# Two gate projections per layer leave the dense phase and join the queue of filler work; modulation sums start earlier; filler budgets change

## The chip, the cores and the metric

The kernel runs on one core of a Trainium2 chip. The metric is the device time of one execution in microseconds (us). TensorE (PE in the rows) does the matrix products, ScalarE (ACT) the activations, casts and exponentials, VectorE (DVE) the elementwise work and the scans, GpSimd (POOL) and SyncE (SP) issue DMAs; ACT issues some too.

## The reference, cut to what matters

Two layers, each on x of 1024 tokens and 1024 channels. A layer modulates a normalised input by sums over `c`, makes one wide projection, runs two attention mixers over it, gates each mixer's output with a SiLU gate, projects, mixes and adds to the residual stream.

```python
mod = jax.nn.silu(c) @ ada_w + ada_b
shift, scale, gate = jnp.split(mod, 3, axis=-1)
h = rms_norm(x, norm_g) * (1 + scale[:, None]) + shift[:, None]
proj = h @ w_in
(sb_q, sb_k, sb_v, sb_z, n_q, k_c, v_c, k_s, v_s, k_w, v_w, n_z, n_g, m_a, m_b) = jnp.split(proj, ...)
a = stick_breaking_attention(heads(sb_q, 8), heads(sb_k, 8), heads(sb_v, 8))
a = a.reshape(B, S, 512) * jax.nn.silu(sb_z)
b = native_sparse_attention(q, kc, vc, ks, vs, kw, vw, n_g)     # 8 heads of 64, 2 key heads
b = b * jax.nn.silu(n_z)
y = jax.nn.sigmoid(m_a) * (a @ w_proj_a) + jax.nn.sigmoid(m_b) * (b @ w_proj_b)
return x + gate[:, None] * (y @ w_out)
```

Stick-breaking weights are a product over the later keys: with z the scaled score, the weight of a key is sigmoid(z) times the product of sigmoid(-z) over the keys between it and the query. The part of the change that matters is `sb_z`: 512 channels whose SiLU multiplies the stick-breaking output, and `mod`, the modulation sums.

## The kernel before

Every float32 product runs as three passes of a split operand (hi times hi, hi times lo, lo times hi), so a unit of a projection (128 channels, 512 tokens, contraction 1024) is 24 matmuls of 128x512: lines L194, L196 and L198 in `mm3_gen`. Four such units (two channel halves `u`, two token halves `half`) make a weight group of 256 columns.

A layer has four stages.

- **Early** (`early`): dense projections whose outputs the sparse attention needs, in code order: compressed keys and values, keys, then a loop of eight token tiles that makes values and branch gates (24 matmuls of 280 columns each, called the v loop below), queries, and at its end the loop over `z` with four groups of SiLU gates (16 units; groups 0 and 1 gate the sparse attention, 2 and 3 the stick-breaking heads). A gate unit is 24 matmuls, a Sigmoid on ACT (L824), a product on DVE (L825) and a store to `SZ` in DRAM. The loop also carries the modulation sums: `mod_part` cuts a sum into eight steps, each a load of 512 KB of `ada_w` (L359, tile `ada`, two buffers) and one DVE instruction over 128x1024 (L362 for the first, L364 for the others). Layer 0 has 24 steps (its own residual gate and the next layer's shift and scale), layer 1 has eight. Two steps go behind each gate unit. When the loop is done, `gate_rows` (L411 on PE, L412 on DVE) and `cols` (L373 on PE, L388 to L391 on DVE) turn the sums into the gate and the modulation vectors.
- **Sparse attention** (`nsa`): a software pipeline of jobs, one for a head and query pair. PE's bursts of a job alternate with queued projection work, the filler: `pump(us)` emits matmuls of the queue `self.fill` until the given amount is spent. The amounts by query pair are written by hand (`nsa_us`, `cmp_us`, and `start_us` before the first job).
- **Stick-breaking** (`sb`): the same pipeline over eight heads with four query pairs each (m0 to m3, 256 to 1024 keys), amounts `sb_us`. On ACT the two sigmoids of the scores (L1239, L1240), on DVE the scan over keys (L1243) and the product (L1244), then PE transposes (L879), ACT and DVE split them (wh, wl) and PE multiplies them with the values (L898, L899).
- **Output** (`output`): loads the mixers' outputs (`AD`, L1333, issued by POOL), splits them, y units (gated projections), output projection, residual, and the norm of the next layer.

The queue before holds 14 groups per layer: queries, keys and values of the stick-breaking heads (six groups) and the eight groups of the mixing gates `m`. By the budgets' own unit, sparse attention spends 8 x (1.97 + 4.16 + 5.85 + 7.05 + 1.48) + 3, about 167 us of it, stick-breaking 8 x 15.02 + 3, about 123 us, against 14 x 20.45 = 286 us of queue (the code reckons a group as 96 matmuls of 0.213 us): the queue before runs out about 4 us before the last job ends. `output` begins when the queue is empty and the last job has been emitted; the scheduler of the framework, not the code alone, decides how far its first products move up among the last head's.

The order within each engine is fixed before the run. An instruction behind a waiting one on the same engine waits too.

Of the kernel before, what the change touches and what calls it, by code (L numbers as in the profile page):

```python
"""Hybrid decoder trunk (stick-breaking attention + native sparse attention) on one Trainium2 core.

float32 products run as three float32r passes: every operand is split exactly into hi + lo
(12 significant bits each), and hi*hi + hi*lo + lo*hi is accumulated in float32 PSUM.  Attention
operands are stacked along the contraction ([hi; lo]) so that two passes carry all four products.
"""
# [14 lines left out]
P = 128  # L21
# [16 lines left out]
def make_consts():  # L38
    """Constants that depend on shapes alone, packed along the free dimension of 128 partitions."""
# [48 lines left out]
class Trunk:  # L88
    def __init__(self, tc, I, O, depth=2, dbg=None):
# [7 lines left out]
        # amount of projection work that is put between the bursts of an attention job, by query pair  # L97
        self.nsa_us = (1.97, 4.16, 5.85, 7.05)
        self.sb_us = (1.34, 2.87, 4.77, 6.04)
        self.cmp_us = 1.48  # L100
        self.start_us = 3.0
        self.tail = 0.15
        # how far dependent transposes are put off
# [11 lines left out]
    # ---------------------------------------------------------------- helpers  # L115
# [17 lines left out]
    def split(self, src, hi, lo):  # L133
        """hi = round12(src) on ScalarE, lo = src - hi on VectorE; src in PSUM or SBUF, float32."""
        nc = self.nc
        nc.scalar.copy(hi, src)  # L136
        nc.vector.tensor_tensor(lo, src, hi.bitcast(F32), ALU.subtract)  # L137

    def rsqrt(self, pool, ss, n, inv, tag, on_pool=False):
        """1/sqrt(ss * inv + EPS) by Newton steps; ss [rows, n]."""  # L140
# [21 lines left out]
    # ---------------------------------------------------------------- weights  # L162
    def load_raw(self, srcs, ncols):
        """srcs(kc) -> list of (DRAM AP [128, 2, ...], column slice) of contraction chunks kc, kc+1."""
# [13 lines left out]
    def split_raw(self, raw):  # L178
        """Tile [128, hi/lo, 2, columns]."""
        n = raw.shape[2]  # L180
        w = self.tl(self.wpool, [P, 2, 2, 280], F32R, "w", bufs=self.wb)
        self.split(raw, w[:, 0, :, :n], w[:, 1, :, :n])
        return w

    def load_group(self, srcs, ncols):
        """The four tiles of a weight group."""
        return [self.split_raw(raw) for raw in self.load_raw(srcs, ncols)]

    def mm3_gen(self, ps, pairs, cost):
        """Three-pass product over pairs ((lhs_hi, lhs_lo), (rhs_hi, rhs_lo)), matmul by matmul."""  # L190
# [21 lines left out]
    def t_unit(self, w, u, half, act, ks=range(KD)):  # L212
        """[128 columns, 512 tokens] = w columns^T @ act^T for one half of the tokens."""
# [4 lines left out]
    def n_unit(self, w, t, act, ncols):  # L218
        """[128 tokens, ncols] = act tokens @ w."""
# [4 lines left out]
    def n_units(self, w, ts, act, ncols):  # L224
        """n_unit of several token tiles, the last chunk of the contraction after the others of all."""
# [9 lines left out]
    # ---------------------------------------------------------------- order of the tensor engine  # L235
    def tick(self, us):
        """us of tensor-engine work have been emitted: emit the deferred work that is due."""
# [4 lines left out]
    def defer(self, us, f):  # L242
        """Emit f once us of tensor-engine work have gone by, so that its operands are ready."""
# [18 lines left out]
    def take(self, ahead=1):  # L262
        """Weights of the next group of the plan; the loads of those that follow are emitted as well."""
# [4 lines left out]
    # ---------------------------------------------------------------- filler: projections run between bursts  # L268
    def pump(self, us):
        """Emit about us microseconds of queued projection work."""  # L270
# [16 lines left out]
    def run_jobs(self, jobs):  # L287
        """jobs: (A bursts, B bursts, us).  The A bursts of a job go between the B bursts of the one before,
        and queued projection work after every burst."""
# [1163 lines left out]
```

## Time and profile before

| | before |
| --- | --- |
| device time, median of 3 | 2231.28 us (2230.01 to 2231.57) |
| span of the profiled execution | 2229.4 us |
| PE busy | 2131.1 us, 96% |
| DVE busy | 1572.0 us, 71% |
| ACT busy | 1129.2 us, 51% |
| PE clock granted in 40 slices | full in nearly all |

The span is that of one profiled execution; the time of the median is 1.9 us more. The rows below come from that execution. A window row gives each engine's busy time in a stretch and the granted clock of TensorE as a share of full speed (1.00 is 2.4 GHz). Matmul ends are modelled, so PE shown busy for a whole window need not be at its best pace; the start of one matmul to the next is the better measure.

### The profile page before, as it was taken

What the parts mean: (1) busy time and instruction counts of PE and PEld (TensorE: products, weight loads), DVE (VectorE), ACT (ScalarE), POOL (GpSimd) and SP (SyncE); (2) the same over time, 40 slices, a digit from 0 to 9 for tenths busy, and PEclk for the clock granted to TensorE, in tenths of its full rate; (3) what the DMA queues carried; (4) which work ended last, traced back from release to release, by engine and by line L of the source; (5) the groups of instructions that cost most, each with busy time, mean ns of one, the idle gap of its engine ahead of it and who ended that gap; (6) DMA issues with size and microseconds to landing.
All of it is one profiled execution on the core that took longest, in us unless ns stands there. A gap on an engine that the chain in (4) does not pass through costs nothing.

```text
span 2229.4 us, 36753 instructions
## 1 busy us (share of the span) xinstructions
PE 2131.1 (96%) x13128; PEld 1841.4 (83%) x13128; DVE 1572.0 (71%) x3714; ACT 1129.2 (51%) x2481; POOL 60.2 (3%) x226
## 2 busy tenths in 40 slices
PE   3999999999999999999999998999999999999999
PEld 3899778988887777789889986889898877777899
DVE  5857558868765877877765852887788487787643
ACT  4533147656665655663443421665666465656410
POOL 2100000000000000000010000000000000001000
PEclk8999999999999999999999999999999999999999
DMA  7435862252116445275455355322522364534433
GB/s 286 131 124 180 250 156 79 88 151 96 66 49 165 127 125 137 86 246 174 159 149 160 97 189 141 94 86 86 142 91 67 92 154 112 149 100 168 150 123 102
DMA packets 239256, 297.04 MB, mean 133 GB/s; under 512 B 21993, under 2 KB 186721, under 8 KB 239073
## 3 DMA queue, kind: packets, MB, share of 16 engines
q1 hardware_dynamic: 198560, 250.65, 36.6%
q10 hardware_dynamic: 36224, 29.37, 5.1%
q0 software_dynamic: 4288, 14.68, 2.0%
q8 instruction: 103, 1.69, 0.3%
q14 instruction: 81, 0.66, 0.1%
HBM read 206.28 MB, written 83.89 MB: 130 GB/s over the span
## 4 chain that ended last, share of the span: by engine, by line
PE 66%; DVE 17%; DMA 7%; issue 5%; ACT 3%; POOL 1%; SPq 0%; ACTq 0%; DVEq 0%; POOLq 0%
PE proj L194 15%; PE proj L198 15%; PE proj L196 15%; PE tr L879 6%; DVE C L1243 4%; PE av L899 4%; PE av L898 3%; PE sc L866 3%; PE sc L867 3%; DVE wl L137 2%; DVE E L1244 2%; DMA ada<-in_ada_w 2%; DVE w L137 2%; DMA kk<-QK 1%; DMA q<-QK 1%
## 5 line engine op out<-in xcount | busy, mean ns | idle before, releaser
L194 PE MATMUL proj<-acthi,w 128*128 128x512 f32 x1312 | 536.9, 409 | 1.3 <-ACT acthi L136 0.7
L196 PE MATMUL proj<-actlo,w 128*128 128x512 f32 x1312 | 536.8, 409 | 0.5 <-DVE actlo L137 0.5
L198 PE MATMUL proj<-acthi,w 128*128 128x512 f32 x1312 | 536.2, 409 | 0.7 <-DVE w L137 0.7
L136 ACT CAST w<-raw 128x512 fp32r<-128x512 f32 (+1 forms) x296 | 183.4, 622 | 230.1 <-PE proj L198 119.0
L137 DVE TENSOR_TENSOR wl<-tr,wh 128x512 fp32r<-128x512 f32 (+2 forms) x432 | 256.6, 610 | 40.8 <-ACT wh L136 38.4
L194 PEld LDWEIGHTS proj<-acthi,w 128*128 128x128 f32 x1312 | 249.4, 190 | 42.1 <-ACT acthi L136 1.6
L196 PEld LDWEIGHTS proj<-actlo,w 128*128 128x128 f32 x1312 | 249.4, 190 | 39.0 <-DVE actlo L137 1.9
L198 PEld LDWEIGHTS proj<-acthi,w 128*128 128x128 f32 x1312 | 249.0, 190 | 37.9 <-DVE w L137 1.2
L137 DVE TENSOR_TENSOR w<-raw,w 128x512 fp32r<-128x512 f32 (+1 forms) x296 | 202.2, 688 | 81.9 <-ACT w L136 79.8
L136 ACT CAST wh<-tr 128x512 fp32r<-128x512 f32 (+2 forms) x432 | 221.2, 527 | 76.1 <-PE tr L879 70.7
L899 PE MATMUL av<-wl,V 128*128 128x256 f32 (+1 forms) x864 | 217.5, 285 | 7.6 <-DVE wl L137 7.3
L194 PE MATMUL proj<-w,acthi 128*128 128x256 f32 (+1 forms) x768 | 221.2, 288 | 2.2 <-DVE s L137 1.7
L198 PE MATMUL proj<-w,actlo 128*128 128x256 f32 (+1 forms) x768 | 221.0, 288 | 0.0
L196 PE MATMUL proj<-w,acthi 128*128 128x256 f32 (+1 forms) x768 | 219.8, 286 | 0.0
L898 PE MATMUL av<-wh,V 128*128 128x256 f32 (+1 forms) x864 | 216.8, 271 | 1.2 <-DVE o L917 0.5
L879 PE MATMUL tr<-ident,E 128*128 128x128 f32 x1152 | 187.3, 276 | 23.7 <-DVE E L1244 23.0
L1243 DVE TENSOR_TENSOR_SCAN C<-C 128x128 f32<-128x128 f32 (+7 forms) x128 | 172.5, 1349 | 53.0 <-ACT C L1239 52.4
L879 PEld LDWEIGHTS tr<-ident,E 128*128 128x128 f32 x1152 | 139.2, 140 | 67.4 <-DVE E L1244 35.0
L899 PEld LDWEIGHTS av<-wl,V 128*128 128x128 f32 x864 | 162.7, 188 | 31.1 <-DVE wl L137 19.3
L866 PE MATMUL sc<-kk,q 128*128 128x512 f32 (+3 forms) x512 | 176.8, 346 | 8.6 <-DVE mx L1079 4.1
L867 PE MATMUL sc<-kk,q 128*128 128x512 f32 (+3 forms) x512 | 175.5, 343 | 0.0
L898 PEld LDWEIGHTS av<-wh,V 128*128 128x128 f32 x864 | 163.0, 189 | 14.0 <-ACT wh L136 3.9
(247 smaller groups left out, 3898.2 us busy)
## 6 DMA issues: line engine op xcount, KB each, us to landing
raw<-in_w_in SPq DMA_DIRECT2D x168, 256.0 KB, 2.9
ada<-in_ada_w SPq DMA_DIRECT2D x48, 512.0 KB, 5.3
kk<-QK SPq DMA_DIRECT2D x48, 512.0 KB, 9.0
q<-QK ACTq DMA_DIRECT2D x64, 256.0 KB, 4.0
QK<-s SPq DMA_DIRECT2D x32, 512.0 KB, 3.0
MD<-sz SPq DMA_DIRECT2D x64, 256.0 KB, 2.6
QK<-s SPq DMA_DIRECT2D x48, 256.0 KB, 3.3
VD<-s SPq DMA_DIRECT2D x48, 256.0 KB, 2.1
```

Of the source, the lines that this page charges most:

```text
L136: nc.scalar.copy(hi, src)
L137: nc.vector.tensor_tensor(lo, src, hi.bitcast(F32), ALU.subtract)
L194: nc.tensor.matmul(ps, lh, rh, start=(x == 0), stop=False)
L196: nc.tensor.matmul(ps, lh, rl, start=False, stop=False)
L198: nc.tensor.matmul(ps, ll, rh, start=False, stop=(x == n - 1))
L866: nc.tensor.matmul(ps, q, k[:, 0, c0:c1], start=True, stop=False)
L867: nc.tensor.matmul(ps, q, k[:, 1, c0:c1], start=False, stop=not masks)
L879: nc.tensor.transpose(pt[:, x * P:x * P + P], b, self.ident)
L898: nc.tensor.matmul(ps[:, c:d], lhsT, hi[:, a:b], start=(first and x == 0), stop=False, skip_group_check=True)
L899: nc.tensor.matmul(ps[:, c:d], lhsT, lo[:, a:b], start=False, stop=(last and x == n - 1), skip_group_check=True)
L1243: nc.vector.tensor_tensor_scan(rev, rev, rev, 1.0, ALU.mult, ALU.bypass)
L1244: nc.vector.tensor_tensor(e[:, 0:nk], e[:, 0:nk], c[:, 1:nk + 1], ALU.mult)
```

## The change

Three edits, one diff (docstrings and comments are blanked in the changed file, so line numbers shift by a few; L824 becomes L840, L1000 becomes L1008, L866 becomes L874, L879 becomes L887).

1. `early` makes only two of the four gate groups. The other two stand first in `self.fill`, as kind "sb" (they have to be done before stick-breaking begins).
2. The filler budgets grow, and the start budget of the sparse attention is 13 us where it was 3; stick-breaking keeps 3.
3. The steps of the modulation sums begin before the v loop: one step per token tile there, then two per gate unit as before, over eight units.

```diff
-        self.nsa_us = (1.97, 4.16, 5.85, 7.05)
-        self.sb_us = (1.34, 2.87, 4.77, 6.04)
-        self.cmp_us = 1.48
-        self.start_us = 3.0
+        self.nsa_us = (2.1, 4.5, 6.3, 7.6)
+        self.sb_us = (1.8, 3.8, 6.2, 7.8)
+        self.cmp_us = 1.6
+        self.start_us = 13.0
...
-    def run_jobs(self, jobs):
+    def run_jobs(self, jobs, start):
...
-            us = jobs[n - 1][2] if n else self.start_us
+            us = jobs[n - 1][2] if n else start
...
             w = self.take()
+            steps = []
+            self.gate, gate_rows = self.mod_gate(l, pool, steps)
+            if l + 1 < self.depth:
+                cols = self.mod_ab(l + 1, pool, steps)
+
+            def mod_steps(n, ins):
+                with tc.issue_after(ins.ins):
+                    for f in steps[:n]:
+                        f()
+                del steps[:n]
+
             for t in range(NT):
                 ps = self.n_unit(w, t, act, 280)
-                self.store_v(ps, t, 8)
+                ins = self.store_v(ps, t, 8)
                 nc.scalar.activation(self.G[:, t, :], ps[:, 256:280], AF.Sigmoid)
+                mod_steps(1, ins)
...
-            for z in range(4):
+            for z in range(2):
                 w = self.take()
-                if z == 0:
-                    steps = []
-                    self.gate, gate_rows = self.mod_gate(l, pool, steps)
-                    if l + 1 < self.depth:
-                        cols = self.mod_ab(l + 1, pool, steps)
                 for u in range(2):
                     for half in range(2):
-                        ps = self.t_unit(w, u, half, act)
-                        s = self.tl(self.stage, [P, 512], F32, "sz")
-                        nc.scalar.activation(s, ps, AF.Sigmoid)
-                        ins = nc.vector.tensor_tensor(s, ps, s, ALU.mult)
-                        with tc.issue_after(ins.ins):
-                            for f in steps[:2]:
-                                f()
-                        del steps[:2]
-                        r0 = z * 256 + u * 128
-                        nc.sync.dma_start(self.SZ[r0:r0 + P, half * 512:half * 512 + 512], s)
+                        mod_steps(2, self.silu_gate(self.t_unit(w, u, half, act), z * 256 + u * P, half))
...
+    def silu_gate(self, ps, r0, half):
+
+        nc = self.nc
+        s = self.tl(self.stage, [P, 512], F32, "sz")
+        nc.scalar.activation(s, ps, AF.Sigmoid)
+        ins = nc.vector.tensor_tensor(s, ps, s, ALU.mult)
+        nc.sync.dma_start(self.SZ[r0:r0 + P, half * 512:half * 512 + 512], s)
+        return ins
...
-            self.run_jobs(jobs)
+            self.run_jobs(jobs, self.start_us)
...
-            self.run_jobs(jobs)
+            self.run_jobs(jobs, 3.0)
...
+                    if what == "z":
+                        self.silu_gate(ps, r0 + u * P, half)
+                    elif what == "qk":
...
+        for z in range(2):
+            self.fill.append(("sb", t_group("z", 512 + z * 256)))
```

DVE at the end of layer 0's early stage, before (rows of the last gate units; `sz` is a gate unit's product, `acc` a step of the sums, `gate` and `Acol` what is made of them):

```order
L364 SCALAR_TENSOR_TENSOR acc_388_2324<-ada_2801,silu_c_86,acc_388_2324 128x1024 [waits DMAHW2_49,DVE_49]
L825 TENSOR_TENSOR sz_2850<-proj_2825,sz_2850 128x512 [waits DMAHW7_49,Activation_49]
L825 TENSOR_TENSOR sz_2879<-proj_2854,sz_2879 128x512 [waits DMAHW4_49,Activation_49]
L825 TENSOR_TENSOR sz_2908<-proj_2883,sz_2908 128x512 [waits DMAHW7_49,Activation_49]
...
L825 TENSOR_TENSOR sz_2937<-proj_2912,sz_2937 128x512 [waits DMAHW0_49,Activation_49]
L412 TENSOR_TENSOR gate_2311<-proj_2941,gate_2311 128x512 [waits PE_49]
```

And in the changed kernel:

```order
L841 TENSOR_TENSOR sz_2659<-proj_2634,sz_2659 128x512 [waits DMAHW4_49,Activation_49]
L364 SCALAR_TENSOR_TENSOR acc_213_1096<-ada_2663,silu_c_86,acc_213_1096 128x1024 [waits DMAHW0_49,DVE_49]
L412 TENSOR_TENSOR gate_1083<-proj_2669,gate_1083 128x512 [waits PE_49]
L364 SCALAR_TENSOR_TENSOR acc_213_1096<-ada_2666,silu_c_86,acc_213_1096 128x1024 [waits DMAHW2_49,DVE_49]
L412 TENSOR_TENSOR gate_1083<-proj_2672,gate_1083 128x512 [waits PE_49]
L388 SCALAR_TENSOR_TENSOR Acol_1087<-proj_2675,vcols_1093 128x8 [waits PE_49]
```

Before, four gate units' products stand behind the last step of the sums; now the last two steps stand behind the last gate unit's product, and the gate's own instructions between and behind them.

ACT at the opening of layer 0's sparse attention, before (`sz` of the last gate unit is done; V and q are loads; `cs`, `E` and `ew` are exponentials, `s` evictions of queries and keys in the queue):

```order
L936 DMA q_2983<-QK_120_589 64x4x256 x2
L936 DMA q_3063<-QK_120_589 64x4x256 x2
L1000 ACT_TABLE_LOAD
L1000 ACTIVATE cs_2991<-cs_2991 128x32
L1091 ACTIVATE E_3067,rs_3070<-E_3067,mx_3069 128x128
L136 CAST s_529_3141<-proj_3027 128x512
```

And in the changed kernel:

```order
L840 ACTIVATE sz_2780<-proj_2755 128x512
L944 DMA q_2848<-QK_120_589 64x4x256 x2
L1008 ACT_TABLE_LOAD
L1008 ACTIVATE cs_2719<-cs_2719 128x32
L840 ACT_TABLE_LOAD
L840 ACTIVATE sz_2829<-proj_2784 128x512
L1008 ACT_TABLE_LOAD
L1008 ACTIVATE cs_2792<-cs_2792 128x64
...
L136 CAST wh_2923<-tr_2919 128x384
L840 ACT_TABLE_LOAD
L840 ACTIVATE sz_2934<-proj_2833 128x512
```

The eight Sigmoids of the queued gate units now stand among the exponentials, and nearly each is preceded and followed by a table load: 15 loads between a layer's first sparse job and its stick-breaking, where there was one (33 in the program, 5 before).

PE in layer 0's last stick-breaking head, before (`proj` with `acthi_28` is filler, `tr` and `av` the head's own work):

```order
L198 MATMUL proj_10843<-acthi_28_137,w_9956 128x512
L194 MATMUL proj_10843<-acthi_28_137,w_9956 128x512
L196 MATMUL proj_10843<-actlo_29_138,w_9956 128x512
L198 MATMUL proj_10843<-acthi_28_137,w_9956 128x512
L194 MATMUL proj_10843<-acthi_28_137,w_9961 128x512
L196 MATMUL proj_10843<-actlo_29_138,w_9961 128x512
L879 MATMUL tr_10894<-ident_85,E_10789 128x128
L879 MATMUL tr_10894<-ident_85,E_10831 128x128 [waits DVE_49]
```

And in the changed kernel, between the scores of that head's second and third query pair (`proj_11020` is the first y unit of the output stage, `acthi_2381` the loaded mixer output):

```order
L874 MATMUL sc_10744<-kk_10378,q_10383 128x512
L875 MATMUL sc_10744<-kk_10378,q_10383 128x512
L877 LDWEIGHTS identb_89
L877 MATMUL sc_10744<-m_strict_90,identb_89 128x128
L194 MATMUL proj_11020<-acthi_2381_10966,w_10320 128x512
L196 MATMUL proj_11020<-actlo_2382_10967,w_10320 128x512 [waits DMASW0_49,DVE_49]
L874 MATMUL sc_10766<-kk_10378,q_10383 128x512 [waits PE_49,Activation_49]
L875 MATMUL sc_10766<-kk_10378,q_10383 128x512
```

Before, queued filler lies among the last head's work to its end and the first y unit comes behind it; now the queue is empty when the head's larger query pairs begin, and 33 matmuls of y units are moved up among them.

## Rows read from the trace of the kernel before

**Rows 1.** The page: busy time and instructions of the engines.
```profile
PE 2131.1 (96%) x13128; PEld 1841.4 (83%) x13128; DVE 1572.0 (71%) x3714; ACT 1129.2 (51%) x2481; POOL 60.2 (3%) x226
```

**Rows 2.** Windows: dense, sparse attention, its opening, stick-breaking (two), v loop, gates.
```profile
core 0: us, PE busy (x) PEld busy (x) DVE busy (x) ACT busy (x) POOL busy (x), PEclk, DMA share, GB/s
220.00:275.00 55.00, 54.23 (x230) 42.70 (x229) 33.59 (x37) 10.78 (x18) 0.00 (x0) 1.00 0.85 261
330.00:385.00 55.00, 54.27 (x339) 46.43 (x338) 47.90 (x160) 41.12 (x104) 0.32 (x2) 1.00 0.26 82
300.00:386.00 86.00, 84.63 (x511) 70.85 (x510) 69.88 (x257) 59.08 (x158) 0.32 (x2) 1.00 0.35 99
715.00:770.00 55.00, 51.55 (x301) 41.81 (x302) 47.23 (x66) 34.41 (x78) 1.48 (x15) 1.00 0.53 139
1815.00:1870.00 55.00, 52.35 (x300) 42.24 (x299) 46.81 (x60) 34.72 (x76) 1.29 (x13) 1.00 0.47 126
105.00:115.00 10.00, 10.00 (x82) 10.00 (x81) 6.84 (x29) 2.21 (x6) 0.00 (x0) 1.00 0.61 187
205.00:215.00 10.00, 10.00 (x45) 8.07 (x44) 5.41 (x7) 1.79 (x3) 0.00 (x0) 1.00 0.96 304
```

**Rows 3.** PE's waits in six stick-breaking heads of layer 0 (719 to 914 us).
```profile
PE tr L879 <- DVE E L1244: 8.3, 13, 1.1
PE av L899 <- DVE wl L137: 2.6, 7, 0.7
```

**Rows 4.** Windows cut at the scans of one stick-breaking head: m0, m1, m2, m3.
```profile
748.40:759.00 10.60, 10.60 (x65) 9.01 (x64) 5.08 (x12) 4.24 (x10) 0.20 (x2) 1.00 0.64 165
759.00:764.70 5.70, 4.83 (x27) 3.38 (x27) 5.32 (x9) 4.71 (x12) 0.20 (x2) 1.00 0.42 132
764.70:773.10 8.40, 7.48 (x42) 5.80 (x41) 7.98 (x11) 6.67 (x15) 0.20 (x2) 1.00 0.29 86
773.10:781.00 7.90, 7.90 (x48) 6.58 (x47) 7.77 (x8) 4.24 (x10) 0.20 (x2) 1.00 0.63 152
```

**Rows 5.** Layer 0's last head: a window, the loads of `AD`, the first y unit.
```profile
940.00:950.00 10.00, 9.02 (x53) 7.05 (x52) 9.91 (x14) 8.59 (x18) 3.69 (x7) 1.00 0.92 293
...
939.48 2.08 POOL L1333 DMA_DIRECT2D actlo<-AD  x3 [5.87 <-PE proj L196]
...
952.54 0.45 PE L194 MATMUL proj<-acthi,w 128*128 128x512 f32 x1
...
953.07 0.39 PE L198 MATMUL proj<-acthi,w 128*128 128x512 f32 x1
953.30 0.40 PE L194 MATMUL proj<-acthi,w 128*128 128x512 f32 x1
```

**Rows 6.** ACT's table loads of sparse attention: busy us, mean ns, idle before.
```profile
L1000 ACT ACT_TABLE_LOAD x2 | 2.6, 1283 | 19.7 <-DMA q<-QK 11.6 <-issue 8.1
```

**Rows 7.** DVE in layer 0's gate loop (195 to 290 us): group, then timeline.
```profile
L364 DVE SCALAR_TENSOR_TENSOR acc<-ada,silu_c,acc 128x1024 f32<-128x1024 f32 x21 | 27.0, 1284 | 20.2 <-DMA ada<-in_ada_w 20.1
...
245.96 1.28 DVE L364 SCALAR_TENSOR_TENSOR acc<-ada,silu_c,acc 128x1024 f32<-128x1024 f32 x1 [0.53 <-DMA ada<-in_ada_w]
...
250.00 1.29 DVE L364 SCALAR_TENSOR_TENSOR acc<-ada,silu_c,acc 128x1024 f32<-128x1024 f32 x1 [1.99 <-DMA ada<-in_ada_w]
```

**Rows 8.** PE's timeline, layer 0: ninth gate unit begins, early tail, first filler.
```profile
240.72 0.39 PE L194 MATMUL proj<-acthi,w 128*128 128x512 f32 x1
...
287.12 1.02 PE L411 MATMUL proj<-acc,ones 128*128 128x512 f32 x2
...
289.65 5.00 PE L373 MATMUL proj<-ones,acc 128*128 128x1 f32 x32
294.51 0.77 PE L194 MATMUL proj<-acthi,w 128*128 128x512 f32 x1
295.09 0.63 PE L196 MATMUL proj<-actlo,w 128*128 128x512 f32 x1
```

**Rows 9.** PE's timeline, opening of layer 1's sparse attention.
```profile
1393.62 1.86 PE L990 MATMUL sc<-KCS,q 128*128 128x16 f32 x8 [7.83 <-DMA q<-QK]
```

More of the change, by code (lines that the diff above doesn't have):

```diff
@@ L136, in split @@
         nc.scalar.copy(hi, src)
-        nc.vector.tensor_tensor(lo, src, hi.bitcast(F32), ALU.subtract)
+        return nc.vector.tensor_tensor(lo, src, hi.bitcast(F32), ALU.subtract)
     def rsqrt(self, pool, ss, n, inv, tag, on_pool=False):
@@ L842, in store_v @@
         src = ps[:, 0:256].rearrange("p (h d) -> p h d", d=HD)
-        self.split(src, vt[:, :, 0:64], vt[:, :, 64:128])
+        ins = self.split(src, vt[:, :, 0:64], vt[:, :, 64:128])
         nc.sync.dma_start(self.VD[t * P:(t + 1) * P, h0:h0 + 4, :], vt.bitcast(F32))
+        return ins
     def load_stack_k(self, pool, row, tag="kk"):
@@ L1258, in t_group @@
                     c = slice(half * 512, half * 512 + 512)
-                    if what == "qk":
+                    if what == "z":
+                        self.silu_gate(ps, r0 + u * P, half)
+                    elif what == "qk":
                         s = self.pair()
```

## Prediction

> **What bounds the kernel now.** I read the page's busy line first: PE works 96% of the span, 2131.1 of 2229.4 us [rows 1]. So a change that moves PE work, and takes none away, can only win where PE idles or lose where it makes PE idle. Then the windows, stage by stage [rows 2]. Dense projections, gates among them, keep PE busy 54.23 of 55 us and sparse attention 54.27 of 55: nothing to win there. Stick-breaking shows 51.55 and 52.35 of 55 in a window of either layer, so about 3 us of idle in 55. A head takes about 33 us (32.6 from 748.4 to 781.0, the sum of the windows in [rows 4]), so a head holds 1.8 us, the idle of those four windows too. What ends it is DVE: in six heads PE waits 8.3 us for the product behind the scan and 2.6 for the low half of the transposed weights [rows 3].
>
> The windows of one head [rows 4] show where. Stretch m0 has PE busy 10.60 of 10.60 and DVE 5.08: bound by PE. Stretches m1 and m2 have DVE busy 5.32 of 5.70 and 7.98 of 8.40, PE idle 0.87 and 0.92: bound by DVE. In m3 both are nearly full.
>
> **Part 1, more filler in stick-breaking.** The two moved groups are 192 matmuls a layer, and a matmul starts 0.23 us after the one before (953.07 to 953.30 [rows 5]); they cost 44.5 us of PE time in either place, so the move itself is worth nothing. The gain is what of the added filler falls into idle PE. The budgets of stick-breaking rise by 0.46, 0.93, 1.43 and 1.76 in their own unit, which counts a matmul 0.213. In m0 the added filler costs its whole time. In m1 and m2 it is 0.46 and 0.93, against 0.87 and 0.92 of idle; in m3 little fits. So at most 1.5 us of a head's 1.8 are won; matmuls are placed in pieces of 0.23 us and waits stay in part, so I take 1.3. For seven heads in two layers: 14 x 1.3 = **-18 us**, range -7 (0.5 a head) to -25 (all 1.8).
>
> **Part 2, the last head.** By the new budgets 190 + 160 us are to be spent on 16 x 20.45 = 327, so the queue is empty some 22 us before the end, when the last head's larger query pairs begin. That head had some 14 us of filler there and gets 33 matmuls of y units, 7.6 us. DVE is its bound already (9.91 of 10 us, PE 9.02 [rows 5]), and now splits for the loads of `AD` come into its queue ahead of the last scans. In this head PE loses 14 - 7.6 = 6.4 us of cover, of which the head shortens by most, since less PE work stands in it; what remains is DVE's own length. I take +2 us a layer, **+4**, range 0 (the y units cover it) to +13 (all 6.4, twice). The loads were issued at 939.48 and the first y unit ran at 952.54, 13 us later without a wait; the order leaves about as much behind the last filler of the first token half, so I count no wait for them.
>
> **Part 3, table loads on ACT.** A Sigmoid among exponentials needs a table load before and one behind it. The order has 14 more a layer, at 1.283 us each [rows 6]: 18.0 us of ACT. They fall into the opening of sparse attention, where ACT is busy 59.08 of 86 us [rows 2]. That makes 77 of 86, so ACT isn't the bound on average; but DVE is busy 69.88 there, PE 84.63, and each pair holds up the exponentials and the splits behind it by 2.6 us, for which PE's transposes and products wait. Seven pairs, if all showed, would be +18 a layer; if filler covers all, 0. I take 3, **+6 us** in both layers, range 0 to +24 (two thirds of the loads).
>
> The rows show the loads alone, behind idle stretches (19.7 us before the two [rows 6]), so they can't show what a switch costs in a busy one. The Trainium skill (ScalarE: Activation LUTs, What ACT_TABLE_LOAD costs) adds a drain of about 1.38 us to each load, 2.66 us for a switch, and in Table sets: the hidden batching unit it asks to do all of one set before switching, which speaks against this change. By that the 14 would be an estimated 37 us a layer, ACT would need 96 us of 86 and bound the opening; the sum would come out 14 us later (10 a layer, less the 6 taken).
>
> **Part 4, the tail of layer 0's early stage.** Before, the steps of the sums ended with the twelfth gate unit, so four units of PE work still lay behind them. Now the last unit is the eighth, which would end at 240.72, where the ninth began before [rows 8]. The steps are paced by their loads: DVE waits 20.1 us for them in 21 steps [rows 7], and is at 4.0 us from one to the next here (245.96 to 250.00). Sixteen are left for eight units either way, since two a unit were issued before too; the fifteenth and sixteenth of that loop run at 245.96 and 250.00 and end at 251.29. PE's last products (L373) need the sixteenth. Half of L373's 5.00 us [rows 8] stands behind it, and a vector step: filler begins at about 255. Before, filler began 294.51 - 287.12 = 7.4 us after the last unit; now 14.3. The difference is **+7 us**, in layer 0 alone: layer 1's eight steps are all done in the v loop. Range +3 (the loads run faster with fewer weights beside them) to +11 (one step more). The matmuls behind the pause run at 0.63 us for 0.40 (295.09 [rows 8]) in either version: one such dip before, one after.
>
> **Part 5, the v loop.** Eight steps, 4.2 MB of loads, come into its 23.4 us (192 matmuls, at 82 in 10 us [rows 2]): 179 GB/s on top of 187. The gate loop shows 304 GB/s with the DMA engines 0.96 busy [rows 2]. At that rate the bytes need (187 + 179) x 23.4 / 304 = 28.2 us, +4.8 a layer; if weights are loaded far enough ahead, 0. DVE has room (6.84 of 10 us, and 1.28 x 8 = 10.3 in 23.4). I take 1.5 a layer, **+3 us**, range 0 to +10.
>
> **Part 6, the opening.** In layer 1 PE waits 7.83 us for the queries' load [rows 9], behind 37 filler matmuls. One would think 13 us of start budget fill that, but the order has the same 37 before those scores: the added ones come behind. So the stall stays: 0, range -8 (it goes) to +4 (loads of q stand behind a gate's Sigmoid on ACT).
>
> **Sum.** -18 + 4 + 6 + 7 + 3 + 0 = +2, against 2229.4: 2231.4. The median lies 1.9 above the profiled execution, so **2233 us**. It is a small difference of large terms, and more of them cost than gain.
>
> **Rivals.**
> - A, stick-breaking's idle goes almost wholly: 1.9 a head with what it holds of pauses shorter than the windows show, -27; last head +2, loads +2, tail +5, v loop 0: -18, **2213 us**. For it: the idle is two thirds waits for DVE of up to 1.1 us [rows 3], which filler behind the waits would cover. Against: m3 and m0 are full. Chance 0.28.
> - B, slower: the table loads decide. The place is the first two sparse heads of each layer, the price half of what 14 loads take, 9 us a layer in place of 3: +12 on the sum, **2245 us**. It decides once ACT's share there passes what its turns with DVE allow; 77 of 86 us is near that. The skill's drain makes the same case stronger. Chance 0.17.
> - C, slower: the sums decide. v loop +9, tail +11: +10, **2243 us**. It decides where loads of weights are queued on SP behind a step's load that waits for its buffer. Chance 0.10.
> - D, the added filler only displaces: DVE stays late by as much, since added evictions of filler stand in its queue, and stick-breaking gains 4 in all: +14, **2247 us**. Chance 0.08.
>
> **How the numbers follow.** The forecast has 0.37, its own range 2226 to 2240. A measurement here can tell about 0.2%, 4.5 us, from no change. Faster by more: nearly all of A and 0.08 of the forecast, 0.34. Within: 0.21 of the forecast and the edges of A and C, 0.26. Slower: 0.08 of the forecast, B, D and most of C, 0.40. The range 2214 to 2251 leaves out a third of A and the far ends of B and D.
>
> **What the profile after would show.** Windows of stick-breaking with PE at 53.5 of 55 and fewer waits behind the scan's product: part 1. A last head with PE idle and DVE at 10 of 10 up to the end: part 2. ACT table loads among exponentials, and PE waiting for wh or wl in the first two sparse heads: part 3. PE waiting for the last step of the sums for 7 us more: part 4. DMA share near 1 and PE short of 10 in the v loop: part 5. The forecast is wrong if sparse attention's opening keeps 54 of 55 and stick-breaking's idle is gone (A), or if ACT is full at the opening (B).

## The result: 1.2% slower, outside the range

The changed kernel takes 2257.26 us (median of 4, 2256.64 to 2261.58) where the kernel before takes 2231.43: the ratio is 1.012 with a 95% interval of 1.0107 to 1.0132. The forecast was 2233, the range ended at 2251. The profiled execution has a span of 2259.8 us, 30.4 above that of before; it is the slowest of the four, so what follows adds up to some 4 us more than the medians show.

The page of the changed kernel, busy time of the engines, answers to [rows 1]:

```profile
PE 2143.6 (95%) x13128; PEld 1854.9 (82%) x13128; DVE 1580.3 (70%) x3714; ACT 1165.9 (52%) x2509; POOL 60.4 (3%) x226
```

The same 13128 matmuls are in the trace, so no PE work was added. ACT is busy 36.7 us longer, which is 28 table loads of 1.283 us and little else. PE is idle 18 us more, and shows 12.5 us more of "busy": matmuls behind some of the pauses run at a lower clock (last section).

To find where, I cut both executions at the same events: the first L411 (end of the gate units), the first filler, the scans of the stick-breaking heads. Windows of layer 0 of the kernel before (start and end, length, busy us of PE, PEld, DVE, ACT, POOL, then granted clock, DMA share, GB/s): sparse attention, head 0, heads 1 to 6, head 7, the output stage up to 1100:

```profile
294.51:697.00 402.49, 395.77 (x2539) 345.08 (x2540) 294.91 (x930) 243.71 (x589) 1.84 (x11) 1.00 0.34 101
697.00:719.50 22.50, 20.40 (x116) 15.44 (x116) 19.86 (x25) 16.94 (x41) 0.69 (x7) 1.00 0.55 134
719.50:913.90 194.40, 183.12 (x1050) 147.73 (x1049) 157.88 (x213) 117.15 (x260) 4.84 (x49) 1.00 0.47 126
913.90:942.40 28.50, 26.98 (x156) 21.83 (x156) 20.61 (x31) 17.35 (x38) 2.58 (x8) 1.00 0.15 49
942.40:1100.00 157.60, 154.97 (x907) 133.47 (x905) 123.22 (x228) 80.81 (x140) 6.36 (x11) 1.00 0.61 202
```

And of the changed kernel:

```profile
258.30:689.10 430.80, 419.78 (x2644) 364.53 (x2643) 305.09 (x941) 266.97 (x611) 1.84 (x11) 1.00 0.33 98
689.10:713.50 24.40, 21.21 (x117) 16.11 (x115) 22.65 (x29) 17.76 (x43) 0.79 (x8) 0.95 0.73 168
713.50:929.80 216.30, 213.90 (x1194) 174.69 (x1193) 160.78 (x214) 123.32 (x271) 4.88 (x49) 1.00 0.44 122
929.80:960.30 30.50, 25.78 (x145) 20.21 (x144) 27.11 (x41) 21.68 (x48) 2.25 (x8) 0.94 0.38 130
960.30:1118.90 158.60, 150.12 (x866) 128.53 (x864) 117.00 (x219) 74.71 (x127) 6.60 (x12) 0.98 0.56 181
```

Length less PE busy is PE's idle. In heads 1 to 6 it falls from 11.3 us to 2.4: the gain that the change aims at is there, and nearly complete. In head 7 it grows from 1.5 to 4.7 though the head has 11 matmuls less, and in the output stage from 2.6 to 8.5, with the clock at 0.94 and 0.98. (The last window ends at the same matmul in both, 1100 and 1118.9.)

Idle time leaves out matmuls that are shown busy and are late. So I also took, for each two matmuls that follow each other, the time from start to start less what such a pair takes in the kernel before when nothing is in the way (the 15th percentile there, by the shapes of the two), and summed it by stage. The sum over all stages differs by 30.9 us, the whole difference of the spans:

| PE time beyond its matmuls' own pace, changed less before, us | layer 0 | layer 1 |
| --- | --- | --- |
| early stage, v loop among it | +2.3 | +2.5 |
| from the last gate unit to the first filler | +6.4 | 0.0 |
| sparse attention, to the first stick-breaking scan | +4.2 | +7.2 |
| stick-breaking head 0 | +2.0 | +1.9 |
| heads 1 to 6 | -11.5 | -12.1 |
| head 7 | +5.4 | +5.6 |
| output stage and what follows it | +9.2 | +7.8 |

So 23.6 us were won in heads 1 to 6, 28.0 lost from the last head on, and 26.5 elsewhere.

**Inside a head.** The four windows of head 2, cut at its scans as in [rows 4], in the changed kernel:

```profile
749.60:761.70 12.10, 11.96 (x70) 9.89 (x69) 5.62 (x12) 3.97 (x11) 0.20 (x2) 1.00 0.74 209
761.70:767.90 6.20, 5.79 (x33) 4.33 (x32) 4.86 (x8) 4.13 (x11) 0.20 (x2) 1.00 0.15 55
767.90:775.60 7.70, 7.70 (x42) 6.18 (x42) 6.37 (x8) 5.15 (x12) 0.20 (x2) 1.00 0.10 36
775.60:784.90 9.30, 9.30 (x53) 7.78 (x52) 9.02 (x9) 5.91 (x14) 0.20 (x2) 1.00 0.50 118
```

PE is the busiest engine in all four now. m0, m1 and m3 got 5, 6 and 5 matmuls more; m2 takes less time than before (7.70 for 8.40) with the same 42 matmuls and DVE busy 6.37 for 7.98, since work of DVE moved out of it, above all into m3 (9.02 us for 7.77). Over six heads the waits of [rows 3] fell to these:

```profile
PE av L907 <- DVE wl L137: 2.1, 6, 0.4
PE tr L887 <- DVE E L1252: 1.0, 1, 1.0
```

**The last head and the output's opening.** PE's waits from 929.8 to 990 us (longest in total first: us, times, longest):

```profile
PE sc L874 <- ACT E L1248: 3.1, 1, 3.1
PE proj L194 <- ACT acthi L136: 2.4, 1, 2.4
PE proj L194 <- DVE gt L1415: 2.1, 1, 2.1
PE av L907 <- DVE wl L137: 1.0, 1, 1.0
```

Three of the four places in PE's timeline (start, length, engine, line, operation, idle before it and what ended it), and behind them two rows of ACT from before the first place:

```profile
940.11 0.40 PE L196 MATMUL proj<-actlo,w 128*128 128x512 f32 x1
943.59 0.50 PE L874 MATMUL sc<-kk,q 128*128 128x512 f32 x1 [3.08 <-ACT E L1248]
...
963.55 0.49 PE L194 MATMUL proj<-acthi,w 128*128 128x512 f32 x1 [2.35 <-ACT acthi L136]
...
971.85 0.80 PE L194 MATMUL proj<-acthi,w 128*128 128x512 f32 x1 [2.10 <-DVE gt L1415]
972.44 0.63 PE L196 MATMUL proj<-actlo,w 128*128 128x512 f32 x1
...
936.81 1.66 ACT L136 CAST acthi<-actlo 128x512 fp32r<-128x512 f32 x3
...
943.05 0.48 ACT L1248 ACTIVATE E<-sc 128x384 f32<-128x384 f32 x1
```

What POOL issued there, in its timeline:

```profile
959.96 0.57 POOL L1345 DMA_DIRECT2D actlo<-AD  x1 [9.38 <-DMA AD<-o]
964.79 2.14 POOL L1411 DMA_DIRECT2D gt<-MD  x4 [4.26 <-DVE o L915]
```

Read from the end. At 971.85 PE waits for the gate product of the first y unit (L1415), which needs the loaded gates `gt`. POOL issues those at 964.79, released by DVE's gating of the last head's output (L915); I read it as a tile that lies where that head's tiles lay. At 963.55 PE waits for the split of a load of `AD` issued at 959.96, released by a store of the last head. At 943.59 PE waits for the sigmoid of the last head's scores (L1248), which ACT ran at 943.05, behind seven casts of the loads of `AD` that it had done from 935.91 on. So the output stage can't do more than some 30 matmuls until the last head is nearly through, and the last head, without filler, is a chain of scan, product, transpose, split and product with DVE busy 27.11 of 30.5 us. Before, the filler of the last head ran beside that chain, and the first y unit began behind the last product without a wait [rows 5].

### The profile page after: what moved, and what is told of

It is laid out like the page before. It is cut to its first block, busy times and chain, and to the rows that moved or that the text cites. A ratio compares the mean times of both kernels' runs of the same rounds, so it can differ in the third digit from the quotient of the medians.

```text
span 2259.8 us, 36759 instructions
## 1 busy us (share of the span) xinstructions
PE 2143.6 (95%) x13128; PEld 1854.9 (82%) x13128; DVE 1580.3 (70%) x3714; ACT 1165.9 (52%) x2509; POOL 60.4 (3%) x226
## 4 chain that ended last, share of the span: by engine, by line
PE 71%; DVE 12%; DMA 7%; ACT 5%; issue 4%; POOL 1%; SPq 0%; ACTq 0%; DVEq 0%; POOLq 0%
PE proj L194 16%; PE proj L196 16%; PE proj L198 16%; PE tr L887 6%; PE av L907 4%; PE av L906 3%; PE sc L874 3%; PE sc L875 3%; DVE C L1251 2%; DMA kk<-QK 2%; DVE wl L137 1%; DMA ada<-in_ada_w 1%; DVE w L137 1%; DVE E L1252 1%; DMA raw<-in_w_in 1%
## 5 line engine op out<-in xcount | busy, mean ns | idle before, releaser
L194 PE MATMUL proj<-acthi,w 128*128 128x512 f32 x1312 | 541.6, 413 | 14.5 <-DVE gt L1415 8.5
L194 PEld LDWEIGHTS proj<-acthi,w 128*128 128x128 f32 x1312 | 251.2, 191 | 52.7 <-DVE gt L1415 9.4
L194 PE MATMUL proj<-w,acthi 128*128 128x256 f32 (+1 forms) x768 | 221.7, 289 | 6.8 <-ACT G L816 5.1
L874 PE MATMUL sc<-kk,q 128*128 128x512 f32 (+3 forms) x512 | 179.4, 351 | 21.2 <-DMA kk<-QK 6.2
L887 PE MATMUL tr<-ident,E 128*128 128x128 f32 x1152 | 189.2, 279 | 9.6 <-DVE E L1252 6.2
L907 PEld LDWEIGHTS av<-wl,V 128*128 128x128 f32 x864 | 163.9, 190 | 31.1 <-DVE wl L137 19.7
L887 PEld LDWEIGHTS tr<-ident,E 128*128 128x128 f32 x1152 | 141.6, 142 | 54.5 <-DVE E L1252 17.8
```

What stands on the lines that cost most here:

```text
L194: nc.tensor.matmul(ps, lh, rh, start=(x == 0), stop=False)
L874: nc.tensor.matmul(ps, q, k[:, 0, c0:c1], start=True, stop=False)
L887: nc.tensor.transpose(pt[:, x * P:x * P + P], b, self.ident)
L907: nc.tensor.matmul(ps[:, c:d], lhsT, lo[:, a:b], start=False, stop=(last and x == n - 1), skip_group_check=True)
```

## Experiments

All times are medians; each ratio is against the kernel before on the same chip.

**e1: the queue lasts to the end.**

```diff
-        self.nsa_us = (2.1, 4.5, 6.3, 7.6)
+        self.nsa_us = (1.97, 4.16, 5.85, 7.05)
-        self.cmp_us = 1.6
-        self.start_us = 13.0
+        self.cmp_us = 1.48
+        self.start_us = 3.0
```

> The changed kernel with the sparse attention's filler budgets and start of before (1.97, 4.16, 5.85, 7.05; 1.48; 3.0), so that the queue still holds 160 us by the budgets' count when stick-breaking begins, which spends 160: the last head is covered to its end. Theory (the empty queue in the last head and at the output's opening costs 28 us of the 26 to 30 lost): PE's idle there is gone, the seven fuller heads gain about 2 us each as six do now, and the time falls to about 2226 (2220 to 2232). Rival (the output's opening waits for its own loads whatever stands before it): the waits behind DVE's gate product and ACT's split of the loaded mixers' output stay, and the time is 2250 or more.

Measured: 2226.47 us (2220.8 to 2228.82), ratio 0.997 (0.9957 to 0.9983). Three settings put back, and the change is 0.3% faster than the kernel before. Head 7 and the 28 us behind it, in its trace (of the fastest of its executions):

```profile
901.00:932.30 31.30, 31.14 (x175) 25.15 (x174) 23.85 (x34) 19.98 (x43) 0.49 (x5) 1.00 0.23 76
932.30:960.00 27.70, 26.72 (x136) 21.71 (x135) 18.65 (x28) 14.91 (x28) 6.27 (x10) 1.00 0.69 247
```

Head 7 takes as long as in the changed kernel (31.3 and 30.5), but with 175 matmuls for 145 and 0.16 us of idle for 4.7. The theory holds. But the run puts back more than the queue's end: by the pace measure, some 30 us of what came back lie from head 7 on, and 11 in sparse attention and head 0, whose budgets it lowered too. e2 and e9 part the two.

**e2: the queue nearly lasts, by smaller stick-breaking budgets.**

```diff
-        self.sb_us = (1.8, 3.8, 6.2, 7.8)
+        self.sb_us = (1.59, 3.35, 5.47, 6.88)
```

> The changed kernel with the stick-breaking budgets times 0.88 (1.59, 3.35, 5.47, 6.88), so that the queue ends about 4 us before the last job, as it did before. Theory (empty queue): the last head and the output's opening lose no more than before (28 us back), the heads before it gain about half of what they gain now (12 in place of 24): about 2242 (2236 to 2248). Rival (output's own loads): 2262 or more, since the heads gain less and nothing comes back.

Measured: 2238.68 us (2234.64 to 2245.01), ratio 1.0031 (1.0019 to 1.0043). From head 7 on, PE loses no more than before in layer 1 and 2 us more in layer 0; heads 1 to 6 gain nearly 6 us a layer, half of what they gain in the changed kernel. The sparse attention's budgets are those of the changed kernel here, so it is the queue's later end, and not a smaller sparse budget, that gave the 28 us back. It isn't as good as e1: sparse attention and head 0 lose 9.5 us by the pace measure, for 4.2 in e1. I read this as filler that goes where PE is full already.

**e9: the kernel before with an empty queue.** One line of the kernel before, nothing else of the change:

```diff
-        self.nsa_us = (1.97, 4.16, 5.85, 7.05)
+        self.nsa_us = (2.2, 4.65, 6.55, 7.88)
```

> The kernel before with one line changed: the sparse attention's budgets raised (2.2, 4.65, 6.55, 7.88), so that its queue too runs empty some 22 us before the end; gate groups, sums and stick-breaking budgets as before. Theory (the empty queue alone costs what the changed kernel lost at the last head and the output's opening): 20 to 28 us slower than before, 2255 (2250 to 2260). Rival (it costs that only together with the changed kernel's other edits): within 5 us of before, 2236 or less.

Measured: 2269.27 us (2266.89 to 2270.59), ratio 1.0161 (1.0146 to 1.0176), 36 us slower, 9 above the expected range. So an early end of the queue alone makes the kernel slower, without any other edit of the change. Head 7 and the 30 us behind it, with the clock at 0.83 in the second:

```profile
938.40:960.00 21.60, 17.92 (x111) 13.87 (x110) 21.44 (x34) 16.18 (x36) 0.87 (x6) 1.00 0.08 25
960.00:990.00 30.00, 23.74 (x103) 19.19 (x102) 21.67 (x33) 12.12 (x23) 4.39 (x8) 0.83 0.66 214
```

By the pace measure 23.4 us of the loss lie from head 7 on, for 28.0 in the changed kernel; 8.4 in sparse attention and head 0, where there was no table load and no queued gate, and some 4 in heads 1 to 6, which I can't account for. Most of the 8.4 is one wait at the end of each layer's sparse attention, for the first keys of stick-breaking (PE sc L866, DMA kk): 4.7 and 4.8 us, for 1.4 and none before. In the changed kernel it is 1.8 and 3.2, so it is a small part of the 15.3 us that those two stages lose there. What the rest is there in detail I didn't settle.

**e4: no table loads.** The queued gate units use Exp in place of Sigmoid, so their stick-breaking gates have other values.

```diff
-    def silu_gate(self, ps, r0, half):
+    def silu_gate(self, ps, r0, half, f=AF.Sigmoid):
...
-        nc.scalar.activation(s, ps, AF.Sigmoid)
+        nc.scalar.activation(s, ps, f)
...
-                        self.silu_gate(ps, r0 + u * P, half)
+                        self.silu_gate(ps, r0 + u * P, half, AF.Exp)
```

> The changed kernel with Exp in place of Sigmoid in the queued gate units (the stick-breaking gates are then other values), which takes away the 28 added table loads, 36 us of ACT, and nothing else. Theory (their cover holds, the loss is elsewhere): within 3 us of the changed kernel, 2254 to 2258. Rival (table loads hold up the exponentials in sparse attention, whose loss outside the opening grew by some 5 us in each layer): 10 us or more faster, 2247 or less.

Measured: 2255.51 us (2254.61 to 2257.01), ratio 1.0098 (1.008 to 1.0117): 1.7 us less than the changed kernel, within the spread of both (by the ratios it is 0.22%, some 5 us, and their intervals overlap). ACT and PE in the first 86 us of sparse attention, the changed kernel and e4:

```profile
258.30:344.30 86.00, 83.74 (x468) 69.25 (x468) 59.75 (x223) 63.40 (x142) 0.32 (x2) 0.98 0.37 98
```

```profile
257.40:343.40 86.00, 84.28 (x471) 70.32 (x472) 62.33 (x227) 49.10 (x135) 0.32 (x2) 0.97 0.39 100
```

ACT is 14.3 us less busy without the loads, and PE does three matmuls more. By the pace measure sparse attention loses 10.2 us in both layers, for 11.4 in the changed kernel. The cover held.

**e3: the modulation sums alone, in the kernel before.** Steps begin in the v loop, one a token tile, all 16 gate units stay.

```diff
...
             for t in range(NT):
                 ps = self.n_unit(w, t, act, 280)
-                self.store_v(ps, t, 8)
+                ins = self.store_v(ps, t, 8)
                 nc.scalar.activation(self.G[:, t, :], ps[:, 256:280], AF.Sigmoid)
+                mod_steps(1, ins)
...
```

> The kernel before with the third edit alone: the steps of the modulation sums begin in the v loop, all 16 gate units stay in the early stage. Theory: it pays for the loads in the v loop, 2.3 and 2.5 us as the stages of the changed kernel show, and has no tail, since eight gate units lie behind the last step: 2236 (2234 to 2238). Rival (the v loop's loss comes from something else in the change): 2231.

Measured: 2236.52 us (2234.07 to 2241.17), ratio 1.0021 (1.001 to 1.0031): 4.4 us slower, as expected. The second 10 us of the loop in e3, and two stretches at and before its stop:

```profile
115.00:125.00 10.00, 6.95 (x32) 6.65 (x31) 3.48 (x5) 1.13 (x4) 0.00 (x0) 0.68 0.69 227
...
114.00:116.00 2.00, 2.00 (x16) 1.92 (x14) 0.69 (x1) 0.59 (x1) 0.00 (x0) 1.00 0.93 337
116.00:118.00 2.00, 0.21 (x2) 0.00 (x0) 0.00 (x0) 0.00 (x0) 0.00 (x0) 1.00 0.84 293
```

PE stops once, for 3.1 us (PE proj L194 behind ACT G L816), and then runs at a lower clock, 0.68 over the 10 us. Over these 10 us the DMA engines are busy 0.69 at 227 GB/s, but in the 4 us from 114 to 118, with most of the stop in them, they are busy 0.93 and 0.84 at 337 and 293 GB/s, about the 0.96 and 304 of [rows 2]; in the kernel before the same two stretches show 0.78 and 0.22. In the changed kernel's trace the same stop is led back to ACT, which waits 3.58 us for a buffer that the stores of the keys (`QK`) hold:

```profile
118.49 0.37 ACT L136 CAST s<-proj 128x256 fp32r<-128x256 f32 x1 [3.58 <-DMA QK<-s]
```

SP issued those stores from 112.60 on, right behind a load of the sums at 112.00, and they took 4.3 us from issue to landing (the median of four). In the kernel before they were issued from 113.29 on with no load ahead and took 2.6, and ACT waited 0.67 us for the same buffer. In e6 below, the sums' loads begin only behind these stores: the stores take 2.4 us there, and PE's stop is 0.2 us. So the loads of the sums delay these stores; whether by the bytes that the engines move or by their place ahead in SP's queue, no run tells.

**e6: the sums spread wider, on e1.** One step behind each of the last six token tiles of the v loop, one behind every second token tile of the queries, the other ten two a gate unit.

```diff
-                mod_steps(1, ins)
+                mod_steps(1 if t > 1 else 0, ins)
...
                     raw.append(self.rope_raw(pool, ps, rt, t, kinds, ss[:, x * 4:x * 4 + 4], "rp", 6))
+                    after(x)
...
-            qk_unit(self.take(), 1, rtq, 1024)
+            qk_unit(self.take(), 1, rtq, 1024, lambda x: mod_steps(x % 2, self.roped))
...
```

> As e1, and the steps of the modulation sums spread wider: one behind each of the last six token tiles of the v loop, one behind every second token tile of the queries, the rest two a gate unit, so that in layer 0 three gate units stand behind the last step. Theory: the tail's 6 us come back, and a part of the v loop's 5; the steps in the query units, where DVE is at 8 of 10, cost 1 or 2: 2219 (2216 to 2222). Rival (the tail is bound by something other than the last steps): as e1, 2226.

Measured: 2221.31 us (2220.35 to 2221.98), ratio 0.9943 (0.9928 to 0.9958), the fastest version. The tail in the changed kernel, then in e6:

```profile
244.62 1.02 PE L411 MATMUL proj<-acc,ones 128*128 128x512 f32 x2
249.09 2.08 PE L411 MATMUL proj<-acc,ones 128*128 128x512 f32 x2 [3.46 <-DVE sz L841]
251.53 6.99 PE L373 MATMUL proj<-ones,acc 128*128 128x1 f32 x32 [0.37 <-DVE gate L412]
258.38 0.77 PE L194 MATMUL proj<-acthi,w 128*128 128x512 f32 x1
```

```profile
244.57 1.02 PE L411 MATMUL proj<-acc,ones 128*128 128x512 f32 x2
246.14 1.13 PE L411 MATMUL proj<-acc,ones 128*128 128x512 f32 x2 [0.55 <-DVE sz L842]
247.10 4.12 PE L373 MATMUL proj<-ones,acc 128*128 128x1 f32 x32
251.08 0.77 PE L194 MATMUL proj<-acthi,w 128*128 128x512 f32 x1
```

From the first L411 to the first filler it is 13.8 us in the one and 6.5 in the other: PE waited for a gate unit's product that stood behind a step of the sums on DVE, then for the last step. The early stage before that tail loses as much as in the changed kernel in layer 0 (2.6 us for 2.3): the stop in the v loop is gone, and waits of 1.5 us (PE tr L762 behind DVE rpt L755, in the query units) and 1.2 us (PE av L718) came in its place.

**e5: queue changed, all budgets of before.** The queue is left with some 37 us when the last job has been emitted.

```diff
-        self.nsa_us = (2.1, 4.5, 6.3, 7.6)
-        self.sb_us = (1.8, 3.8, 6.2, 7.8)
-        self.cmp_us = 1.6
-        self.start_us = 13.0
+        self.nsa_us = (1.97, 4.16, 5.85, 7.05)
+        self.sb_us = (1.34, 2.87, 4.77, 6.04)
+        self.cmp_us = 1.48
+        self.start_us = 3.0
```

> The changed kernel with all filler budgets of before, those of stick-breaking too: the two gate groups are in the queue, the heads get no more filler than before, and some 37 us of the queue are left when the last job has been emitted and run densely behind it. Theory: nothing of the gain in the heads (12 a layer) and nothing of the loss behind the empty queue; what is left is the early stage's loss of 11 us and 1 or 2 at the opening of stick-breaking: 2243 (2239 to 2247). Rival (the move itself gains or costs by other ways, table loads or evictions): outside that.

Measured: 2254.95 us (2250.39 to 2257.96), ratio 1.0092 (1.0077 to 1.0107), 12 above the forecast: a miss. Heads 1 to 7 lose what they lost before, to 0.3 us each, as expected. The early stage and the tail lose 13.0 more than before by the pace measure, and sparse attention 2.3 in layer 0 and 1.8 in layer 1. What I had not reckoned with is the output stage, 7.2 us worse in layer 0 and 1.6 in layer 1. POOL issues the loads of `AD` at

```profile
957.88 2.07 POOL L1345 DMA_DIRECT2D actlo<-AD  x3 [42.42 <-PE proj L198]
```

after 42 us behind PE: they go where the layer's input lies, which the leftover filler reads to its end. So too much queue is bad as well, by another tile's life. That the miss is made of these is a reading of one trace; its profiled execution lies 1.3 us above the median.

**e7: the first gate loads issued by SP, on the changed kernel.**

```diff
-            self.gt = (nc.gpsimd if ku < 2 else nc.sync).dma_start(
+            self.gt = nc.sync.dma_start(
```

> The changed kernel with the first y units' loads of the mixing gates issued by SP, not by POOL, where they stood behind a load that waited for the last head's store. Theory (the missing filler is the cause, the late gate loads only a part of how it shows): the wait of PE behind DVE's gate product goes, 2 us in layer 0 and up to 5 in layer 1: 2251 (2249 to 2255). Rival (POOL's queue is the cause of the whole loss): 2240 or less; rival (no part in it): 2257.

Measured: 2265.55 us (2262.92 to 2269.86), ratio 1.0144 (1.0127 to 1.0161): 8 us slower, against all three expectations. In layer 0 SP issued the loads only behind the last head's last store, later than POOL had:

```profile
969.62 8.94 SPq L1411 DMA_DIRECT2D gt<-MD  x6
```

PE's wait for the gate product is then 7.4 us in layer 0 and 8.2 in layer 1, for 2.1 and 5.1 in the changed kernel, 8.4 more in all, about the loss. So it is shown, by the wrong sign, that PE restarts by the landing of these loads; an issue earlier than POOL's wasn't tried.

**e8: the start budget, on e6.** 13 us at the outset, the heads' budgets cut by as much.

```diff
-        self.nsa_us = (1.97, 4.16, 5.85, 7.05)
+        self.nsa_us = (1.85, 3.92, 5.51, 6.64)
-        self.start_us = 3.0
+        self.start_us = 13.0
```

> As e6, with the start budget of the sparse attention at 13 and its heads' budgets cut by as much (1.85, 3.92, 5.51, 6.64), so that the same filler is left for stick-breaking. Theory (a start budget covers the first job's waits behind the first compressed scores, 1.7 and 1.5 us in e6, and some short ones): 3 to 5 us faster than e6, 2217 (2215 to 2219). Rival (the filler is only missing later): as e6, 2221.

Measured: 2225.97 us (2224.72 to 2229.97), ratio 0.9966 (0.995 to 0.9982): no gain, and by medians 4.7 slower than e6 (on another chip; the ranges of the times don't overlap, the intervals of the ratios do). The first 90 us of sparse attention lose 0.8 and 1.8 us less than in e6; the rest of it, with less filler in its jobs, 6.8 and 5.2 more. I read this as follows: sparse attention isn't bound by PE as firmly as its 54.27 of 55 [rows 2] made me think, and PE was full there because the filler was just enough.

## Why the prediction was wrong, step by step

- **Part 1 (heads), right in kind, somewhat short.** 18 us forecast for seven heads, 1.3 each; heads 1 to 6 of both layers gained 23.6, 2.0 each, rival A's 1.9 in this part. Head 0, the seventh, lost 3.9, so the seven together came to 19.7. The place (m1 and m2, waits for DVE) was right; the way was right in m1 alone, since in the head shown m2 lost its idle without any added matmul.
- **Part 2 (the last head), the step that failed.** The term was +4, range 0 to +13; it measured 11.0 in head 7 and 17.0 from there on. Two statements in it were wrong. "In this head PE loses 14 - 7.6 = 6.4 us of cover, of which the head shortens by most": it didn't shorten, 30.5 us for 28.5 from first to last scan, since DVE's chain sets its length. DVE is busy 27.11 us there for 20.61; seven splits of loads of `AD` (4.5 us) and four of weights (2.7) stand in it that were not there before. And "I count no wait for them": I looked at the loads of `AD` for the nsa half, and took the 13 us between their issue and the first y unit for enough. The loads that ended last were others: the quarter that needs the last heads' stores, and the gates, which wait for the last head's tiles. What hid them before was the filler, a cover that I removed without asking what else it hid. With the queue lasting longer (e2) the 28 us are gone, and with the kernel before cut short (e9) 23.4 us appear in the same places.
- **Part 3 (table loads), too dear.** +6 forecast, 1.7 by e4's median, not clear of its spread. Rival B falls: ACT came to 63.40 of 86 us, not 77.
- **Part 4 (the tail), right.** +7 forecast, +6.4 measured, and e6 gives it back. The last step ran at 252.00 and the first filler at 258.38; the forecast had 250.00 and 255, 2.0 and 3.4 us earlier, some 2 of it by the v loop's loss.
- **Part 5 (the v loop), right in size, and in the main in cause.** +3 forecast, 4.8 by the stages and 4.4 by e3. Over 10 us of the loop DMA is busy 0.69 and not at its full rate, as the sum assumed for all of the loop; but it is nearly full for the 4 us in which the keys' stores land late, and that one stop, with the lower clock behind it, is most of the loss. Rival C named SP's queue, for weights; a place in that queue may have a part here, for stores.
- **Part 6 (the opening), right.** The wait of [rows 9] is 6.1 us for 7.8, and the first 90 us of sparse attention lose 2.2 and 2.7 less.
- **What no part had:** sparse attention behind its opening and head 0, 6.4 and 2.0 in layer 0 and 9.9 and 1.9 in layer 1. e1, with the sparse budgets of before, loses 4.2 us over the two stages in both layers, for 15.3 in the changed kernel, and e9 loses 8.4 over the two stages with larger sparse budgets alone, most of it in the wait for the first keys. Larger budgets in a full stage were counted as free, because PE's work is conserved; they were not. How the 15.3 us come about stays open.
- **The sum.** With the measured 28.0 in place of 4 the forecast's own terms would have given 2257. That this is the measured median is in part luck: the other terms are off by -5.6 (heads 1 to 6), +9.3 (sparse attention and head 0, for the 6 of Part 3), -0.6 and +1.8, together +4.9, and the profiled execution lies 4.3 above its median. Slower by more than 0.2% had the largest chance, 0.40, but by rivals B, C and D; the case that decided wasn't among them.

## What to carry to other kernels

A queue of filler hides more than the stage that it was tuned for: when budgets are raised, work out where the queue runs out, and price that place as the chain without any filler, with the next stage's first loads behind it. Here cover was needed most at the end, where the loads of the next stage waited for tiles and stores of this one; so take filler from the stage that has PE full (here sparse attention) and keep it for the last job, as e1 does with three settings. And a budget that leaves too much is no safe side either, if the next stage's loads wait for what the filler reads.

## What the runs showed of the hardware

- **A switch of ACT's table cost its load and little more in this busy stretch.** The changed kernel at 311 us (start, length, engine, line, operation):

```profile
311.08 0.56 ACT L136 CAST wh<-tr 128x512 fp32r<-128x512 f32 x1
311.66 1.28 ACT L840 ACT_TABLE_LOAD   x1
312.96 0.60 ACT L840 ACTIVATE sz<-proj 128x512 f32<-128x512 f32 x1
313.45 0.47 ACT L136 CAST wh<-tr 128x384 fp32r<-128x384 f32 x1
313.94 1.28 ACT L1099 ACT_TABLE_LOAD   x1
315.24 0.72 ACT L1099 ACTIVATE E<-E,mx 128x512 f32<-128x512 f32 x1
```

The load begins 0.02 us after the cast before it ends (311.08 + 0.56 = 311.64), and the Sigmoid 0.02 us after the load. So it is some 1.3 us for a switch, and e4, without the 28 loads, has ACT busy 37.1 us less, 1.33 for each. The Trainium skill (ScalarE: Activation LUTs, What ACT_TABLE_LOAD costs) adds a drain of about 1.38 us to each load. It doesn't show here; the measurement decides, and by it the 14 us that the prediction worked out from the drain fall away.

- **A pause of PE can cost more than its length.** After the 2.10 us wait at 971.85 the next matmul starts 0.59 us later (971.85 to 972.44), and those behind it show 0.63 us each for 0.40 at the full clock, until 975.00; started 0.43 and not 0.23 us apart, they take some 1.5 us more. It doesn't follow every pause. Here are the stretches behind two waits for a sigmoid of the last head's scores, 3.08 us long in layer 0 (until 943.59) and 2.39 in layer 1 (until 2047.46):

```profile
944.00:948.00 4.00, 4.00 (x17) 3.38 (x16) 3.94 (x8) 3.59 (x9) 0.20 (x2) 0.57 0.02 4
2048.00:2052.00 4.00, 3.58 (x22) 2.62 (x22) 3.94 (x8) 3.95 (x11) 0.20 (x2) 1.00 0.05 7
```

Behind the first the granted clock is 0.57 of full speed, a mean that lies near the lower level of 1.2 GHz; behind the second it is 1.00, 2.4 GHz.
